# A two-layer hybrid DiT block on one core: the overflow branch, the order of the last two experts, and three adaLN blocks

## The chip, the cores and the metric

The kernel runs on one NeuronCore of a Trainium2 chip. The metric is the device time of one execution in microseconds (us); the time before is the median of three runs.

## What is computed

Two layers (l = 0, 1) run over 256 latent tokens and, in layer 0, 256 context tokens, with D = 1024. Cut to what matters:

```python
for l in range(2):
    mod = silu_c @ w_ada[l] + b_ada[l]                  # adaLN: 6 vectors of 1024, for latent and for context
    u = (x * (1 + sc1) + sh1) @ w_in[l]                 # one projection, 1024 x 4096
    a = hgrn2_mixer(u)                                  # gated linear recurrence, 4 heads, both directions
    b = na_mixer(u)                                     # 2-D neighbourhood attention, 8 heads
    x = layer_norm(ALPHA * x + g1 * (concat(a, b) @ w_out[l]))
    f = grouped_moe(x * (1 + sc2) + sh2)                # 16 experts, 2 per token: silu(t@Wg)*(t@Wu) @ Wd
    x = layer_norm(ALPHA * x + g2 * f)
```

All of it is float32. The adaLN product of a layer is cut into 24 blocks of 256 columns, 1 MB of w_ada each.

## The kernel before

**Layer 0's front** (`front`, L470). The projection is worked off in 16 chunks of 256 columns. The weights of a chunk (1 MB) are loaded by SP into a tile `w8` (`wload`, L194, DMA at L199), and are then split in four pieces into a high and a low float32r half: `wh` by ACT (L421), `wl` by POOL or DVE (L422). TensorE multiplies three products for each piece (L426, L427, L428; the results are named `pscm` where channels lie on the partitions, `pstm` where tokens do). adaLN blocks use the same tiles: a `w8` is loaded from w_ada, and `ada_blocks` (L367) issues 8 matmuls a block into `psada` (L377), an ACT copy (L380), then a transpose pair `ptada` (L384) and two DVE operations (L395). One such group can hold several blocks if they are of the same kind; the kinds change at blocks 8, 12 and 20 of a layer (`fill`, L399). **The ring of `w8` tiles has three buffers (NWP = 3), used in the order of the program**, and SP issues its loads in that order too. How many blocks are worked behind which chunk stands in a table, `FILL0` for layer 0: 18 in all. They go on into the blocks of layer 1 once those of layer 0 are done. After a chunk the attention of finished heads (`ats` L880/L881, `atp` L901, `ato` L912, with `ex` on DVE at L891) and the recurrence (`hgB` L727, `hgX` L744 to L784, `hgt` L661) is worked in between; a scheduler weaves them on TensorE.

**The experts** (`moe`, L1303). Each expert loads gate and up as four tiles of 1 MB (`load(e, "gu")`, half of them for `gu(e, k0)`, half for `gu(e, k1)`) and down as two (`load(e, "d")`), all by SP at L1335. The tiles come from `wslot()`: a ring `we` of seven, later slots of `mw` and others. Tokens are gathered (`xg`, POOL L1345), transposed (`ptx` L1354), multiplied (`pgA` L1369), put through silu and product (L1386 to L1388), transposed (`pth` L1394, `hdT` L1396), multiplied down (`pdA` L1406, `pdB` L1412), copied to `y` (ACT L1419, DVE L1425) and scattered to DRAM as `yD` (POOL L1433). `y` has a single buffer. The loop over the experts works gate and up of expert e + 1 ahead of down of expert e; with `early` set, down of the last but one expert goes between the two halves of the last one's gate and up. `early` holds in layer 1 only.

**Behind the experts.** If an expert got more tokens than it has room for, `overflow(l)` works them off. A flag (DVE maximum L1521, matmul `pfl` L1523, `values_load` L1526) is read by each engine in both layers, and `tc.If(fv)` (L1531) branches at the end of each `moe`. Ahead of this branch, in layer 0, six adaLN blocks of layer 1 are loaded (L1486, NADA = 6): three into `w8` tiles, three into `mw` tiles; `fill(6, True)` works them. Then `combine` (L1535) loads `yD` back (L1555), scales it (ACT L1579, DVE L1580), transposes it (`ptf` L1568) and makes the input of layer 1.

Of the kernel before, what the change touches and what calls it, by code (L numbers as in the profile page):

```python
# [40 lines left out]
NADA = 6  # L41
NFREE = 14, 13
SPL = ({3: "GVGV", 4: "GGVG", 6: "GGVG", 7: "GGVG", 13: "GVGG", 14: "GVGV"}, {1: "VVGV", 2: "VVGV", 3: "VGVG", 4: "GVGG"})
NF, NTOT, NBT = 1, 1, 3
FILL0 = (0, 0, 0, 2, 2, 2, 2, 0, 2, 0, 2, 2, 0, 2, 0, 2)
# [140 lines left out]
class Emit:  # L186
# [55 lines left out]
    def open(self, name, side="left", **k):  # L242
        p = self.tc.tile_pool(name=f"{name}{self.l}", bufs=1, side=side, reuse_waits="tile", **k)
        return p, p.__enter__()
# [17 lines left out]
    def run(self):  # L262
# [48 lines left out]
        self.late = self.open_step = None  # L311
        for l in range(2):
            self.l = l
            self.layer(l)
            if self.stop and self.stop.startswith(f"L{l}"):
                return

# [112 lines left out]
    def layer(self, l):  # L430
        self.t0 = 0 if l == 0 else CTX
        self.T = (NT - self.t0) // P
        psa, self.psA = self.open("psA", space=PSUM)
        psb, self.psB = self.open("psB", space=PSUM)
        if l == 0:
            self.late, self.fp = self.open("late", "left")
            self.xsplit_alloc()
        early, self.tp = self.open("early", "right")
        self.front(l)
        self.close(early)  # L440
        rp, self.rp = self.open("rt", "right")
        we, self.wep = self.open("we", "right")
        self.close(psb)
        self.close(psa)
        psp, self.ps = zip(*(self.open(f"ps{i}", space=PSUM) for i in range(2)))
        self.psA = self.psB = None
        self.rA, self.rB = [0, 1], [3]
        sums = self.w_out(l)
        self.close(self.late)
        moe, self.ep = self.open("moe", "left")  # L450
        self.ln1_end(1, *sums)
        self.moe(l)
        self.close(moe)
        if l == 0:
            self.l = 1
            self.late, self.fp = self.open("late", "left")
            self.xsplit_alloc()
            self.l = 0
            self.combine(l)
        self.close(psp[1])  # L460
        self.close(psp[0])
        self.close(we)
        self.close(rp)
# [6 lines left out]
    def front(self, l):  # L470
# [9 lines left out]
        if l == 0:  # L480
# [6 lines left out]
            def blocks(p):  # L487
                for b in (2 * p, 2 * p + 1):
                    self.todo[b - self.todo[0][1]] = (l, b, self.wload(A["wada"][l, b])[:])
# [34 lines left out]
            def load(p):  # L524
# [6 lines left out]
                if p == 0:  # L531
# [771 lines left out]
    def moe(self, l):  # L1303
# [97 lines left out]
        def down(e):  # L1401
# [12 lines left out]
            y = et([P, D], "y")  # L1414
# [43 lines left out]
        flag = self.rt([P, 1], "flag", 1, I32)  # L1458
        for e in range(NE):
# [3 lines left out]
            early = l == 1 and e == NE - 2  # L1463
# [15 lines left out]
            if e == NE - 1 and l == 0:  # L1479

                for i in range(NADA):
                    if i < NWP:
                        w = self.wp.tile([P, 2048], F32, tag="w8", name="wa")[:]
                    else:
                        w = ep.tile([P, 2, 1024], F32, tag="mw", bufs=NMW, name="wa").rearrange("p a b -> p (a b)")
                    nc.sync.dma_start(w, self.A["wada"][self.todo[i][:2]])  # L1486
                    self.todo[i] = self.todo[i][:2] + (w,)
# [31 lines left out]
            if e == 3:  # L1519
                fl16 = self.rt([P, 1], "fl16", 1, F16)  # L1520
                V.tensor_reduce(fl16[:], R["ov"][:, :T], axis=AX.XY, op=ALU.max)  # L1521
                pfl = self.bank(7, "pfl")
                mm(pfl[:, 0:1], self.one16[:], fl16[:], start=True, stop=True)  # L1523
                V.tensor_copy(flag[:], pfl[:, 0:1])
                fv = nc.values_load(flag[0:1, 0:1], min_val=0, max_val=P)
        if l == 0:  # L1526
            self.rA = self.rB = [4, 5, 6, 7]
            self.fill(NADA, True)
        else:
            self.finish()  # L1530
        with self.tc.If(fv):  # L1531
            self.overflow(l)
# [236 lines left out]
```

## Time and profile before

| | |
|---|---|
| median of three runs | 1316.8 us (1316.08 to 1317.06) |
| profiled execution | 1317.83 us, span 1316.1 us |
| TensorE, VectorE, ScalarE, GpSimd busy | 1199.3, 590.2, 413.8, 334.4 us |
| layer 0: front, w_out and routing, experts | to 367, to 450, to 697 us |
| handover: end of layer 0's experts to layer 1 | 697 to 742 us |
| layer 1: front to routing, experts, end | to 1055, to 1288, to 1316 us |

The stages are read off the timeline of the profiled execution. In the rows below, a row of a timeline gives the start in us, the duration, the engine, the line, the operation with its output and inputs, their shapes and the number of instructions that are taken together; brackets hold the idle time of the engine before it and what ended that. A PE row of float32 counts two passes for each matmul. SPq rows are the DMA issues of SP; several on one line are taken together, from the start of the first to the end of the last.

### The profile page before, as it was taken

The numbers are of one execution on the slowest core, as the hardware profiler recorded it, in microseconds if no ns is written. First come the engines' busy times: TensorE is split into PE (matmuls) and PEld (weight loads), VectorE is DVE, ScalarE is ACT, GpSimd is POOL, SyncE is SP. The second block draws the span as 40 slices with busy tenths as digits, with TensorE's granted clock in tenths as the row PEclk, the third lists the DMA queues.
The fourth block names the chain that finished last, engine by engine and source line by source line (L and its number), as shares of the span: only waits on it lengthen the run. The fifth ranks groups of instructions, "written<-read, shape, count | busy, mean of one in ns | idle before, by whom it ended". The sixth has DMA issues, their size and how long they took to land. (4 is left out here: it accounts for less than half of the span.)

```text
span 1316.1 us, 22763 instructions
## 1 busy us (share of the span) xinstructions
PE 1199.3 (91%) x8919; PEld 747.6 (57%) x8919; DVE 590.2 (45%) x1397; ACT 413.8 (31%) x905; POOL 334.4 (25%) x349
## 2 busy tenths in 40 slices
PE   6989999988999799998997999998889899999984
PEld 4778767667788334333332688876667734333321
DVE  2466554786735414121111756364785524322214
ACT  2233254452544114111112653354345312001011
POOL 2233243323223101111000534353343311111001
PEclk9999999999999799999998999998999889999996
DMA  8794325313385799999998524354335799999993
GB/s 299 250 313 189 122 89 197 116 52 108 124 332 188 266 374 375 386 395 384 412 404 298 227 101 167 115 192 152 131 116 213 314 352 380 389 404 402 421 413 151
DMA packets 67684, 339.32 MB, mean 258 GB/s; under 512 B 10003, under 2 KB 17907, under 8 KB 31856
## 3 DMA queue, kind: packets, MB, share of 16 engines
q1 hardware_dynamic: 54016, 315.74, 62.1%
q0 software_dynamic: 5936, 12.58, 2.9%
q10 hardware_dynamic: 7616, 9.44, 2.2%
q8 instruction: 74, 1.21, 0.4%
q14 instruction: 42, 0.34, 0.1%
HBM read 322.80 MB, written 20.45 MB: 261 GB/s over the span
## 5 line engine op out<-in xcount | busy, mean ns | idle before, releaser
L422 POOL TENSOR_TENSOR wl<-w,wh 128x512 fp32r<-128x512 f32 x121 | 166.4, 1389 | 188.5 <-ACT wh L421 171.7
L1369 PE MATMUL pgA<-we,xgT 128*64 128x512 f32 x688 | 165.2, 613 | 2.7 <-DMA we<-in_wgu_dram 2.7
L426 PE MATMUL pscm<-xh,wh 128*128 128x512 f32 (+1 forms) x320 | 119.1, 376 | 3.3 <-ACT wh L421 2.3
L427 PE MATMUL pscm<-xl,wh 128*128 128x512 f32 (+1 forms) x320 | 120.7, 379 | 0.7 <-POOL xl L1603 0.5
L428 PE MATMUL pscm<-xh,wl 128*128 128x512 f32 (+1 forms) x320 | 118.6, 375 | 2.8 <-POOL wl L422 2.6
L421 ACT ACTIVATE wh<-w 128x512 fp32r<-128x512 f32 x160 | 96.5, 626 | 50.4 <-PE pscm L427 18.7
L1369 PEld LDWEIGHTS pgA<-we,xgT 128*64 128x64 f32 x688 | 48.1, 140 | 95.1 <-issue 84.9
L427 PE MATMUL pstm<-wl,xh 128*128 128x256 f32 x320 | 92.6, 290 | 3.4 <-DVE wl L422 1.8
L428 PE MATMUL pstm<-wh,xl 128*128 128x256 f32 x320 | 91.9, 287 | 0.0
L426 PE MATMUL pstm<-wh,xh 128*128 128x256 f32 x320 | 91.6, 287 | 0.0
L1433 POOL DMA_INDIRECT yD<-y,ss x25 | 23.0, 921 | 244.6 <-DVE y L1421 79.9
L1406 PE MATMUL pdA<-we,hdT 128*64 128x512 f32 x320 | 77.6, 619 | 3.3 <-DMA we<-in_wd_dram 3.2
L1369 PE MATMUL pgA<-mw,xgT 128*64 128x512 f32 x336 | 77.5, 598 | 0.0
L1360 DVE COPY xgT<-ptx 128x256 f32<-128x256 f32 (+1 forms) x32 | 15.4, 482 | 134.2 <-PE ptx L1354 91.1
L426 PEld LDWEIGHTS pscm<-xh,wh 128*128 128x128 f32 x320 | 61.3, 193 | 13.8 <-ACT wh L421 2.4
L428 PEld LDWEIGHTS pscm<-xh,wl 128*128 128x128 f32 x320 | 61.5, 193 | 12.5 <-POOL wl L422 3.4
L427 PEld LDWEIGHTS pscm<-xl,wh 128*128 128x128 f32 x320 | 61.9, 194 | 11.2 <-POOL xl L1603 1.6
L1387 DVE SCALAR_TENSOR_TENSOR hid<-hid,pgA 128x256 f32<-128x256 f32 x32 | 13.5, 421 | 115.2 <-ACT hid L1386 115.1
L427 PEld LDWEIGHTS pstm<-wl,xh 128*128 128x128 f32 x320 | 61.4, 192 | 5.4 <-POOL wl L422 2.2
L1386 ACT ACTIVATE hid<-pgA 128x256 f32<-128x256 f32 x32 | 12.3, 383 | 159.5 <-PE pgA L1369 159.5
L428 PEld LDWEIGHTS pstm<-wh,xl 128*128 128x128 f32 x320 | 61.5, 192 | 1.1 <-issue 0.8
L426 PEld LDWEIGHTS pstm<-wh,xh 128*128 128x128 f32 x320 | 61.4, 192 | 0.5
(394 smaller groups left out, 2358.9 us busy)
## 6 DMA issues: line engine op xcount, KB each, us to landing
we<-in_wgu_dram SPq DMA_DIRECT2D x86, 1024.0 KB
mw<-in_wgu_dram SPq DMA_DIRECT2D x42, 1024.0 KB
w<-in_wada_dram SPq DMA_DIRECT2D x41, 1024.0 KB
we<-in_wd_dram SPq DMA_DIRECT2D x40, 1024.0 KB
w<-in_win_dram SPq DMA_DIRECT2D x29, 1024.0 KB
mw<-in_wd_dram SPq DMA_DIRECT2D x24, 1024.0 KB
w<-in_wout_dram SPq DMA_DIRECT2D x11, 1024.0 KB
wa<-in_wada_dram SPq DMA_DIRECT2D x6, 1024.0 KB
```

What stands on the lines that cost most here:

```text
L421: self.nc.scalar.activation(hi, src, AF.Copy)
L422: leng.tensor_tensor(lo, src, hi.bitcast(F32), op=ALU.subtract)
L426: mm(out, lh, rh, start=first, stop=False, **k)
L427: mm(out, lh, rl, start=False, stop=False, **k)
L428: mm(out, ll, rh, start=False, stop=last, **k)
L1360: V.tensor_copy(t[:, 0:4, :c], src)
L1369: mm(pA[64 * j:64 * j + 64, :], xgT[e][:, k, 0:64], wk[:, 512 * j:512 * j + 512], start=(k == 0), stop=(k == KT - 1), skip_group_check=Tru ...
L1386: S.activation(h, ps[:, :n], AF.Tanh, scale=0.5)
L1387: V.scalar_tensor_tensor(h, h, 1.0, ps[:, :n], op0=ALU.add, op1=ALU.mult)
L1406: mm(dA[64 * j:64 * j + 64, :], hdT[e][:, kb, 0:64], wk[:, 512 * j:512 * j + 512], start=(kb == 0), stop=(kb == 3), skip_group_check=True, ...
L1433: G.indirect_dma_start(out=self.yD[l][:], out_offset=bass.IndirectOffsetOnAxis(ap=idx, axis=0), in_=y[:c], in_offset=None, bounds_check=2 ...
```

## The change

There are four edits.

- The branch at the end of each layer is gone. In layer 0 the DVE maximum of the overflow marks is kept in a tile (`over`); in layer 1 it is joined with that layer's, and one flag is made. Behind both layers one `tc.If` runs the whole pass again, with `slow` set, and only this second pass calls `overflow`.
- `early` holds in both layers: in layer 0, too, down of expert 14 (and the load of its weights) goes ahead of the second half of gate and up of expert 15. The last expert's `y` in layer 0 comes from the ring of two `xg` tiles.
- Behind the experts of layer 0, three adaLN blocks are worked in place of six (NAFTER = 3), and their tiles are `we` tiles.
- The three others are worked in layer 0's front: `FILL0` has 3 in place of 2 behind chunks 8, 11 and 13.

```diff
@@ constants
 NADA = 6
+NAFTER = 3
-FILL0 = (0, 0, 0, 2, 2, 2, 2, 0, 2, 0, 2, 2, 0, 2, 0, 2)
+FILL0 = (0, 0, 0, 2, 2, 2, 2, 0, 3, 0, 2, 3, 0, 3, 0, 2)
@@ run
+        self.over = c([P, 1], "over")
+        self.slow = False
         for l in range(2):
             self.l = l
             self.layer(l)
...
+        with tc.If(self.fv):
+            self.slow = True
+            self.x = [self.xtile(h) for h in range(2)]
+            for l in range(2):
+                self.l = l
+                self.layer(l)
@@ layer
         self.moe(l)
+        if self.slow:
+            self.overflow(l)
@@ moe, down
-            y = et([P, D], "y")
+            y = et([P, D], "xg", NXG) if l == 0 and e == NE - 1 else et([P, D], "y")
@@ moe, loop over the experts
-            early = l == 1 and e == NE - 2
+            early = e == NE - 2
...
-                for i in range(NADA):
-                    if i < NWP:
-                        w = self.wp.tile([P, 2048], F32, tag="w8", name="wa")[:]
-                    else:
-                        w = ep.tile([P, 2, 1024], F32, tag="mw", bufs=NMW, name="wa").rearrange("p a b -> p (a b)")
-                    nc.sync.dma_start(w, self.A["wada"][self.todo[i][:2]])
-                    self.todo[i] = self.todo[i][:2] + (w,)
+                for i in range(NAFTER) if self.todo else ():
+                    t = self.todo[i][:2]
+                    w = self.wep.tile([P, 2, 1024], F32, tag="we", bufs=NWE, name="wa").rearrange("p a b -> p (a b)")
+                    nc.sync.dma_start(w, self.A["wada"][t])
+                    self.todo[i] = t + (w,)
...
-            if e == 3:
+            if e == 3 and l == 0:
+                V.tensor_reduce(self.over[:], R["ov"][:, :T], axis=AX.XY, op=ALU.max)
+            if e == 3 and l == 1 and not self.slow:
                 fl16 = self.rt([P, 1], "fl16", 1, F16)
                 V.tensor_reduce(fl16[:], R["ov"][:, :T], axis=AX.XY, op=ALU.max)
+                V.tensor_tensor(fl16[:], fl16[:], self.over[:], op=ALU.max)
                 pfl = self.bank(7, "pfl")
                 mm(pfl[:, 0:1], self.one16[:], fl16[:], start=True, stop=True)
...
         if l == 0:
             self.rA = self.rB = [4, 5, 6, 7]
-            self.fill(NADA, True)
+            self.fill(NAFTER, True)
         else:
             self.finish()
-        with self.tc.If(fv):
-            self.overflow(l)
```

**SP's loads at chunks 8 to 11 of layer 0.** `in_win` is a chunk, `in_wada` an adaLN block; the number behind `w8_` counts the tiles of the ring, so that tiles whose numbers differ by three share a buffer. Before (chunk 8 is `w8_21`, chunk 9 `w8_24`):

```order
L199 DMA w8_21_1741<-in_win_dram 128x2048
L199 DMA w8_22_1814<-in_wada_dram 128x2048
L199 DMA w8_23_1824<-in_wada_dram 128x2048
L199 DMA w8_24_1841<-in_win_dram 128x2048
L199 DMA w8_25_1947<-in_win_dram 128x2048
L199 DMA w8_26_2021<-in_wada_dram 128x2048
L199 DMA w8_27_2031<-in_wada_dram 128x2048
```

and after (chunk 9 is `w8_25`, and its buffer is that of `w8_22`):

```order
L200 DMA w8_21_1742<-in_win_dram 128x2048
L200 DMA w8_22_1815<-in_wada_dram 128x2048
L200 DMA w8_23_1825<-in_wada_dram 128x2048
L200 DMA w8_24_1835<-in_wada_dram 128x2048
L200 DMA w8_25_1852<-in_win_dram 128x2048
L200 DMA w8_26_1958<-in_win_dram 128x2048
L200 DMA w8_27_2032<-in_wada_dram 128x2048
L200 DMA w8_28_2050<-in_wada_dram 128x2048
```

One block more stands ahead of chunk 9, which moves chunk 9 to the buffer of the group's first block.

**TensorE at chunk 9.** `psada` is the adaLN group behind chunk 8, `ato` attention, `ptada` the transpose pair of the group, and `pscm` chunk 9. Before:

```order
L377 MATMUL psada_1813<-w8_22_1814,scw_89 32x256
L912 MATMUL ato_1592<-pT_1680,bv_0_603 64x256 x7
L377 MATMUL psada_1813<-w8_22_1814,scw_89 32x256 x7
L377 MATMUL psada_1813<-w8_23_1824,scw_89 32x256 x8
L384 MATMUL ptada_1836<-ct_69,adasb_1467 128x4 x2
L426 MATMUL pscm_1859<-xh0_0_118,wh_0_1843 128x512
L427 MATMUL pscm_1859<-xl0_0_126,wh_0_1843 128x512
L428 MATMUL pscm_1859<-xh0_0_118,wl_0_1844 128x512
```

and after:

```order
L387 MATMUL psada_1814<-w8_22_1815,scw_89 32x256
L924 MATMUL ato_1593<-pT_1681,bv_0_604 64x256 x7
L387 MATMUL psada_1814<-w8_22_1815,scw_89 32x256 x7
L387 MATMUL psada_1814<-w8_23_1825,scw_89 32x256 x8
L387 MATMUL psada_1814<-w8_24_1835,scw_89 32x256 x8
L394 MATMUL ptada_1847<-ct_69,adasb_1468 128x4 x2
L436 MATMUL pscm_1870<-xh0_0_119,wh_0_1854 128x512
L437 MATMUL pscm_1870<-xl0_0_127,wh_0_1854 128x512
L438 MATMUL pscm_1870<-xh0_0_119,wl_0_1855 128x512
```

The third block's 8 matmuls are put between the second's and `ptada`; nothing else moves there.

**TensorE at chunk 12.** `psada` is the last block behind chunk 11, `hgB` and `hgX` the recurrence, `ats` attention scores, `pscm` chunk 12. Before:

```order
L377 MATMUL psada_2303<-w8_30_2314,scw_89 32x256 x8
L384 MATMUL ptada_2326<-ct_69,adasb_2041 128x4 x2
L727 MATMUL hgB_2345<-uq_1990,ks_2343 64x64 x8
L744 MATMUL hgX_2358<-Q2_0_2331,KC_2356 64x64 x8
L426 MATMUL pscm_2520<-xh0_0_118,wh_0_2504 128x512
L427 MATMUL pscm_2520<-xl0_0_126,wh_0_2504 128x512
L428 MATMUL pscm_2520<-xh0_0_118,wl_0_2505 128x512
L426 MATMUL pscm_2520<-xh1_0_119,wh_0_2504 128x512
L427 MATMUL pscm_2520<-xl1_0_127,wh_0_2504 128x512
L428 MATMUL pscm_2520<-xh1_0_119,wl_0_2505 128x512
L744 MATMUL hgX_2373<-Q2_0_2331,KC_2371 64x64 x8
```

and after:

```order
L387 MATMUL psada_2322<-w8_32_2343,scw_89 32x256 x8
L394 MATMUL ptada_2355<-ct_69,adasb_2060 128x2 x2
L739 MATMUL hgB_2374<-uq_2001,ks_2372 64x64 x8
L756 MATMUL hgX_2387<-Q2_0_2360,KC_2385 64x64 x8
L892 MATMUL ats_2605<-ks0_0_2300,qs0_0_2259 128x256
L893 MATMUL ats_2605<-kl0_0_2302,qs0_0_2259 128x256
L892 MATMUL ats_2614<-ks1_0_2301,qs1_0_2260 128x256
L893 MATMUL ats_2614<-kl1_0_2303,qs1_0_2260 128x256
L756 MATMUL hgX_2402<-Q2_0_2360,KC_2400 64x64 x8
L436 MATMUL pscm_2549<-xh0_0_119,wh_0_2533 128x512
L437 MATMUL pscm_2549<-xl0_0_127,wh_0_2533 128x512
L436 MATMUL pscm_2576<-xh0_0_119,wh_0_2533 128x512
```

Four attention matmuls now stand where chunk 12 began, and chunk 12 begins behind the second `hgX`. Chunk 14 has moved in the same way behind chunk 13's blocks.

**TensorE at the end of layer 0's experts.** `pgA` with `xgT_0_6335` (before) or `xgT_0_6355` (after) is gate and up of expert 15, `pdA` with two tiles of weights is down of expert 14 and then of 15, `pth` the transposes of expert 15's hidden values, `psada` the adaLN blocks behind them. Before:

```order
L1369 MATMUL pgA_6418<-we_6400,xgT_0_6335 64x512 x4
L1369 MATMUL pgA_6418<-we_6412,xgT_0_6335 64x512 x4
L1369 MATMUL pgA_6418<-mw_6414,xgT_0_6335 64x512 x4
L1369 MATMUL pgA_6418<-mw_6416,xgT_0_6335 64x512 x4
L1406 MATMUL pdA_6449<-mw_6445,hdT_0_6431 64x512 x4
L1394 MATMUL pth_6465<-ct_69,hid_0_6441 128x128 x2
L1406 MATMUL pdA_6449<-mw_6447,hdT_0_6431 64x512 x4
L1406 MATMUL pdA_6486<-mw_6470,hdT_0_6468 64x512 x4
L1406 MATMUL pdA_6486<-mw_6472,hdT_0_6468 64x512 x4
L377 MATMUL psada_6502<-wa_6474,scw_89 32x256 x8
L377 MATMUL psada_6502<-wa_6476,scw_89 32x256 x8
L377 MATMUL psada_6502<-wa_6478,scw_89 32x256 x8
```

and after:

```order
L1381 MATMUL pgA_6442<-we_6420,xgT_0_6355 64x512 x4
L1381 MATMUL pgA_6442<-we_6432,xgT_0_6355 64x512 x4
L1418 MATMUL pdA_6457<-mw_6434,hdT_0_6455 64x512 x4
L1418 MATMUL pdA_6457<-mw_6436,hdT_0_6455 64x512 x4
L1381 MATMUL pgA_6442<-mw_6438,xgT_0_6355 64x512 x4
L1381 MATMUL pgA_6442<-mw_6440,xgT_0_6355 64x512 x4
L1406 MATMUL pth_6485<-ct_69,hid_0_6481 128x128 x2
L1418 MATMUL pdA_6500<-mw_6490,hdT_0_6488 64x512 x4
L1418 MATMUL pdA_6500<-mw_6492,hdT_0_6488 64x512 x4
L387 MATMUL psada_6516<-wa_6494,scw_89 32x256 x8
L387 MATMUL psada_6516<-wa_6496,scw_89 32x256 x8
L387 MATMUL psada_6516<-wa_6498,scw_89 32x256 x8
```

Down of expert 14 has moved ahead of the second half of gate and up of expert 15, and the branch that stood behind the third adaLN block (with three blocks more behind it) is gone. In layer 1, `pfl` has moved behind the first transposes `ptx`.

## Rows read from the trace of the kernel before

**Rows 1.** The page: busy time, share of the span and instructions of each engine.
```profile
PE 1199.3 (91%) x8919; PEld 747.6 (57%) x8919; DVE 590.2 (45%) x1397; ACT 413.8 (31%) x905; POOL 334.4 (25%) x349
```

**Rows 2.** Windows: bounds, length; PE, PEld, DVE, ACT, POOL busy; PEclk; DMA share; GB/s.
```profile
165.00:243.00 78.00, 75.30 (x455) 54.20 (x455) 43.69 (x102) 42.32 (x97) 33.15 (x31) 1.00 0.36 130
243.00:300.00 57.00, 52.39 (x432) 38.66 (x429) 45.21 (x96) 25.46 (x58) 14.10 (x13) 0.97 0.31 105
300.00:367.00 67.00, 60.41 (x538) 51.67 (x537) 44.94 (x103) 31.62 (x77) 22.38 (x33) 0.97 0.31 113
...
697.00:719.00 22.00, 12.76 (x118) 5.21 (x116) 0.92 (x3) 3.65 (x7) 2.40 (x5) 0.82 0.69 245
...
1055.00:1288.00 233.00, 221.97 (x1422) 82.42 (x1422) 60.95 (x137) 27.03 (x70) 27.77 (x33) 0.98 1.00 395
```

**Rows 3.** Timeline of TensorE, 186 to 197: the group behind chunk 8, then chunk 9.
```profile
192.01 1.93 PE L377 MATMUL psada<-w,scw 128*32 128x256 f32 x30
193.87 0.61 PE L384 MATMUL ptada<-ct,adasb 128*128 128x4 f32 x4
194.34 0.48 PE L426 MATMUL pscm<-xh,wh 128*128 128x512 f32 x1
...
194.88 0.40 PE L428 MATMUL pscm<-xh,wl 128*128 128x512 f32 x1
```

**Rows 4.** Timeline of SP's DMA issues, 160 to 260: one chunk's load.
```profile
208.60 0.33 SPq L199 DMA_DIRECT2D w<-in_win_dram  x1
```

**Rows 5.** Timelines of ACT and POOL, 207 to 221: that chunk's split.
```profile
214.36 1.68 ACT L421 ACTIVATE wh<-w 128x512 fp32r<-128x512 f32 x3 [2.19 <-DMA w<-in_win_dram]
...
215.07 5.01 POOL L422 TENSOR_TENSOR wl<-w,wh 128x512 fp32r<-128x512 f32 x4 [5.80 <-PE pscm L428]
```

**Rows 6.** Waits of SP, 60 to 367: us in total, times, longest.
```profile
SPq L199 <- DMA w<-in_win_dram: 41.8, 9, 8.5
```

**Rows 7.** Timeline of TensorE, 240 to 270: recurrence behind chunk 11's blocks.
```profile
244.40 0.84 PE L744 MATMUL hgX<-Q,KC 128*64 128x64 f32 x16
```

**Rows 8.** Timelines of TensorE in the front: the first and last of six idle gaps.
```profile
266.07 0.67 PE L783 MATMUL hgX<-Q,K 128*128 128x256 f32 x2 [1.96 <-DVE K L796]
...
357.25 0.77 PE L661 MATMUL hgt<-ct,ah 128*128 128x128 f32 x4 [1.70 <-DVE ah L658]
```

**Rows 9.** Windows, columns as above: two stretches of the front.
```profile
180.00:196.00 16.00, 14.21 (x97) 9.29 (x97) 11.65 (x20) 8.46 (x17) 8.27 (x8) 1.00 0.21 66
...
262.00:278.50 16.50, 13.52 (x74) 11.05 (x72) 12.97 (x26) 7.50 (x19) 4.41 (x3) 0.90 0.19 65
```

**Rows 10.** Timeline of all engines, 684 to 720: the end of layer 0's experts.
```profile
693.39 0.38 ACT L1386 ACTIVATE hid<-pgA 128x256 f32<-128x256 f32 x1 [6.50 <-PE pgA L1369]
...
695.47 0.38 ACT L1396 ACTIVATE hdT<-pth 128x256 f32<-128x256 f32 x1 [1.69 <-PE pth L1394]
...
698.64 3.65 PE L1406 MATMUL pdA<-mw,hdT 128*64 128x512 f32 x16 [1.34 <-ACT y L1419]
698.87 0.90 POOL L1433 DMA_INDIRECT yD<-y,ss  x1 [9.07 <-ACT y L1419]
...
704.01 1.19 ACT L1419 ACTIVATE y<-pdA 64x512 f32<-64x512 f32 x2 [5.42 <-DMA yD<-y,ss]
705.48 0.90 POOL L1433 DMA_INDIRECT yD<-y,ss  x1 [5.72 <-ACTq L1531]
...
712.60 5.16 SPq L1555 DMA_DIRECT2D y<-yD  x8
...
717.57 0.72 ACT L1579 ACTIVATE y<-y,gt 128x512 f32<-128x512 f32 x1 [2.36 <-DMA y<-yD]
```

**Rows 11.** The same timeline: TensorE behind the branch.
```profile
709.26 5.49 PE L377 MATMUL psada<-wa,scw 128*32 128x256 f32 x48 [4.24 <-PEq L1531]
```

**Rows 12.** Windows, columns as above: behind the last scatter's issue.
```profile
705.00:710.00 5.00, 0.76 (x12) 0.45 (x12) 0.00 (x0) 0.21 (x1) 0.90 (x1) 0.77 0.92 343
```

**Rows 13.** Timeline of all engines, 1046 to 1058: the flag of layer 1.
```profile
1056.13 0.19 PE L1523 MATMUL pfl<-fl,one 128*128 128x1 f16 x1 [2.75 <-DVE fl L1521]
```

More of the change, by code (lines that the diff above doesn't have):

```diff
@@ L242, in open @@
     def open(self, name, side="left", **k):
-        p = self.tc.tile_pool(name=f"{name}{self.l}", bufs=1, side=side, reuse_waits="tile", **k)
+        p = self.tc.tile_pool(name=f"{name}{self.l}{'s' * self.slow}", bufs=1, side=side, reuse_waits="tile", **k)
         return p, p.__enter__()
@@ L487, in blocks @@
             def blocks(p):
-                for b in (2 * p, 2 * p + 1):
+                for b in (2 * p, 2 * p + 1) if self.todo else ():
                     self.todo[b - self.todo[0][1]] = (l, b, self.wload(A["wada"][l, b])[:])
@@ L530, in load @@
                     nc.sync.dma_start(sub(raw[c], 2 * p), A["win"][l, c][:, 2 * p:2 * p + 2])
-                if p == 0:
+                if p == 0 and self.todo:
                     self.todo[1] = (l, 1, self.wload(A["wada"][l, 1])[:])
@@ L1457, in moe @@
         gu(0, k1)
-        flag = self.rt([P, 1], "flag", 1, I32)
         for e in range(NE):
@@ L1518, in moe @@
                     nc.sync.dma_start(self.ln2[:, i], self.A["ln2"][i:i + 1, :].partition_broadcast(P))
-            if e == 3:
+            if e == 3 and l == 0:
+                V.tensor_reduce(self.over[:], R["ov"][:, :T], axis=AX.XY, op=ALU.max)
+            if e == 3 and l == 1 and not self.slow:
                 fl16 = self.rt([P, 1], "fl16", 1, F16)
                 V.tensor_reduce(fl16[:], R["ov"][:, :T], axis=AX.XY, op=ALU.max)
+                V.tensor_tensor(fl16[:], fl16[:], self.over[:], op=ALU.max)
                 pfl = self.bank(7, "pfl")
                 mm(pfl[:, 0:1], self.one16[:], fl16[:], start=True, stop=True)
+                flag = self.cp.tile([P, 1], I32, name="flag")
                 V.tensor_copy(flag[:], pfl[:, 0:1])
-                fv = nc.values_load(flag[0:1, 0:1], min_val=0, max_val=P)
+                self.fv = nc.values_load(flag[0:1, 0:1], min_val=0, max_val=P)
         if l == 0:
             self.rA = self.rB = [4, 5, 6, 7]
-            self.fill(NADA, True)
+            self.fill(NAFTER, True)
         else:
             self.finish()
-        with self.tc.If(fv):
-            self.overflow(l)
     def combine(self, l):
```

## The prediction

> **What bounds the kernel now.** I read the page first: TensorE is busy 91% of the span [rows 1]. So I cut the span into stages and read each one's busy times, granted clock and DMA share [rows 2]. In layer 0's front, 165 to 367, TensorE is busy 75.30 of 78, 52.39 of 57 and 60.41 of 67 us with the DMA engines at about a third: work put on TensorE here lengthens the stage, and a load is late only where its buffer came free late. At the handover between the layers, 697 to 719, TensorE is busy 12.76 of 22 us: a chain of scatter, landing and load sets the pace. The experts of layer 1 run with the DMA engines full (1.00). Then I read, on the timelines, the three places where the change works: the front of layer 0 (three adaLN blocks come in), the handover (three go out, the branch goes, the last experts are turned round) and the start of layer 1's experts (the flag).
>
> The sum is made against the profiled execution, 1317.8 us; the median is 1316.8, so 1.0 is taken off at the end. About 0.2%, or 2.6 us, is what a measurement of this kernel can tell from no change: "same" is 1314.2 to 1319.4.
>
> **Part 1: three blocks more in layer 0's front.** 30 passes of psada take 1.93 us [rows 3], 0.064 each; a block is 8 matmuls in two passes each, 1.03. Three blocks: **+3.1**, on the bound engine. At chunk 10 two blocks now fall into different kinds, so one more transpose pair stands on TensorE, by the row of ptada 0.61: **+0.6**. The small ACT and DVE operations of that group lie beside TensorE's work.
>
> The larger cost is a wait that before does not have. Projection chunks and adaLN blocks share one ring of three buffers (w8). Before, a chunk behind a group of two blocks takes the buffer of the chunk ahead of them, and its load waits for that chunk's split alone; chunk 9's first matmul stands at 194.34 with no idle time ahead of it [rows 3]. After, the third block takes that buffer, and chunk 9 the first block's: its load waits until that block's matmuls are done. The order of the change shows only the two other blocks and a transpose pair between. Block one is done at about 193.0 (192.01 and half of the 30 passes). What a load takes from issue to use shows where one runs alone: issued 208.60 [rows 4], first split 214.36 [rows 5], 5.76, and this split is three for 1.68, so about 0.6 each; the first matmul needs one. 193.0 + 5.76 + 0.6 = 199.4, while TensorE is ready at 194.34 + 1.03 = 195.4: 4.0. The lower half is four for 5.01 on POOL [rows 5], 1.25, and the third matmul asks for it 0.54 behind the first (194.88 against 194.34): 0.7 more. **+4.7**. Bounds: the loads that SP itself waited for took 41.8/9 = 4.6 on the mean and 8.5 at most [rows 6], so 4.6 + 0.6 - 2.4 = 2.8 and 8.5 + 0.6 - 2.4 + 0.7 = 7.4 (2.4 is 195.4 - 193.0). I take the lone load, since the queues are as empty here.
>
> Chunk 12 stands so behind chunk 11's blocks, chunk 14 behind chunk 13's; there the new order has recurrence between: two blocks 2.06, ptada 0.5, three groups hgB and hgX at about 0.7 (0.84 with the tail [rows 7]), four attention matmuls of 256 columns like psada's 0.13, 0.5. That covers 5.2 of 6.4, so 1.2 or 1.3 each: **+2.6**. Bounds 0 (these loads go a little sooner than the others) and 6 (that work slides behind the wait).
>
> What is given back: later in the front TensorE stands idle for DVE or POOL, six times, 1.96 in the first and 1.70 in the last, together 7.7 [rows 8]. Work that is late anyway shortens a gap only where what it waits for was not held up by TensorE too; most of these are DVE results of a projection chunk, which come later as well. I take a third, **-2.7**; bounds 0 and -7.7.
>
> [...]
> [...]
>
> Front: 3.1 + 0.6 + 4.7 + 2.6 - 2.7 + 1.7 = **+10.0**.
>
> **Part 2: the handover.** TensorE does 24 block matmuls here in place of 48, and meets no branch, but neither is on the path: what it must do next are transposes of y, which wait for DVE. The branch held TensorE 4.24 us [rows 11], while the path went through DMA. On the path is the last expert's output. Its ACT copy waits 5.42 us for the scatter of the expert before, because both use one buffer; its scatter is issued at 705.48; SP's first load of y goes at 712.60, when that has landed [rows 10]. After, the last expert has another buffer and the expert before it is finished first. So the last gate/up half ends later by one down projection: 693.39 + 3.65 = 697.0. The chain from there to the transposed hidden values, 693.39 to 695.47 + 0.38, 2.46, was beside a down projection and now lies open: 699.5. Down 3.65: 703.15. The ACT copy starts at 703.2 in place of 704.01: -0.8. The last scatter landed 6.2 us after the end of its issue (706.38 to 712.60), the one before it 4.2 (699.77 to 704.01): beside the last ran two adaLN loads of 1 MB that SP issued behind the branch, with the DMA share at 0.92 [rows 12]. After, no such load is left for then: -2.0. Together **-2.8**. Bounds: -0.8 (landing unchanged) and -5.2 (and the whole of the 2.36 that ACT waits for the load of y [rows 10]). I take the middle one, since it has a measured pair of landings.
>
> **Part 3: the flags.** pfl leaves its place ahead of layer 1's first ptx, where TensorE waited 2.75 us for it [rows 13]; ptx could go up to 1.8 sooner. But the stage behind is DMA-bound [rows 2] and its loads are released elsewhere: **-0.3**, bounds 0 and -1.8. Layer 0's flag matmul, the DVE maximum added and the single branch at the end cost nothing: other work of the experts hides the first two, and the branch stands at the end either way.
>
> **Sum.** 10.0 - 2.8 - 0.3 = +6.9; 1317.8 + 6.9 - 1.0 = **1323.7**.
>
> **The rivals.**
> *Same (about 1316).* The front's waits only move idle time: all 7.7 us [rows 8] come back and no clock falls. 3.1 + 0.6 + 4.7 + 2.6 - 7.7 - 2.8 - 0.3 = +0.2, 1317.0; with chunks 12 and 14 covered, 1314.4. For it: the new order puts attention matmuls into the recurrence. Against it: five of the six gaps wait for DVE chains that begin with TensorE results.
> *Faster (1313).* One mechanism, the empty queue at the handover: scatter and load of y both land without the adaLN loads beside them, -5.2. It decides from the point where the front's net cost is under 2.9; at 2.0 it gives 2.0 - 5.2 - 0.3 = -3.5. For it: the chain at 697 to 719 is all DMA latency, at a DMA share of 0.92. Against it: the front must lose less than the 3.7 of its bare matmuls.
> [...]
> *The flag is set.* Then the whole pass runs again, over 2600. TensorE goes from the branch to psada [rows 11] with nothing of the overflow between, so layer 0's flag is clear.
>
> **How the numbers follow.** Forecast, 1319.5 to 1326: 0.44. Clock, above that: 0.15. Same: 0.20. Faster: 0.20. Rerun: 0.01. Slower is 0.44 + 0.15 + 0.01 = 0.60. The range takes in the forecast, the same, most of the clock's case and the near half of the faster: 1312.5 to 1329.
>
> **What would show it.** A stop of about 4 us on TensorE behind three psada blocks at about 195, ended by chunk 9's split or its load; SP waiting for psada there; two stops under 2 us near the recurrence of chunks 12 and 14; a clock below 1.00 behind the first. At the handover, the first load of y about 2.8 us sooner, reckoned from the last expert's first gate/up matmuls, and no branch before the end. It is wrong if the front from 165 to 367 grows by less than 4 us, or if the handover shrinks by more than 5.

## The result: 19 us slower, beyond the range

| | before | changed |
|---|---|---|
| median | 1316.9 us (4 runs, 1316.08 to 1319.82) | 1335.9 us (4 runs, 1330.42 to 1339.20) |
| the same pair again, in another session | 1315.2 us (13 runs) | 1335.3 us (4 runs) |
| profiled execution, first and second trace: span | 1316.1, 1315.2 us | 1328.5, 1333.0 us |

The ratio is 1.0136 (95% interval 1.0099 to 1.0173), in the second session 1.0146 (1.0090 to 1.0202). The forecast was 1323.7 with a range up to 1329. The sign was right; the size was not.

The views that answer to [rows 2] are windows of the changed kernel's trace. The columns are bounds, length, busy time and count of PE, PEld, DVE, ACT and POOL, granted clock, DMA share and GB/s. The stretches are cut at the same events in every kernel: the second group of recurrence matmuls in layer 0, the third, the first matmul of w_out, the first expert, and then the handover from the last expert's first gate and up matmul to the first transposes of y, layer 1's front, and TensorE's last matmul to the end.

```profile
122.80:249.10 126.30, 119.40 (x847) 88.08 (x847) 65.28 (x155) 52.44 (x118) 35.84 (x36) 0.96 0.39 140
249.10:372.10 123.00, 104.83 (x910) 83.76 (x909) 80.50 (x177) 52.38 (x121) 36.54 (x38) 0.96 0.34 118
...
704.70:735.80 31.10, 19.59 (x123) 7.03 (x120) 3.51 (x9) 4.58 (x9) 3.32 (x6) 0.85 0.50 180
813.70:1017.50 203.80, 187.26 (x1493) 150.13 (x1489) 131.00 (x294) 87.01 (x193) 84.56 (x80) 0.99 0.41 148
1312.30:1328.50 16.20, 0.00 (x0) 0.00 (x0) 6.53 (x14) 2.48 (x4) 2.10 (x2) 0.50 0.19 71
```

The same stretches of the kernel before, cut anew:

```profile
125.00:243.90 118.90, 113.78 (x811) 84.84 (x810) 68.34 (x153) 53.61 (x119) 41.85 (x40) 0.99 0.39 144
243.90:358.00 114.10, 103.52 (x894) 82.29 (x893) 83.12 (x177) 51.15 (x119) 31.63 (x35) 0.97 0.27 92
...
686.30:719.20 32.90, 23.48 (x171) 8.69 (x167) 3.52 (x9) 5.21 (x10) 3.32 (x6) 0.88 0.79 298
795.80:1005.40 209.60, 191.89 (x1493) 152.74 (x1489) 131.83 (x294) 87.14 (x193) 84.65 (x80) 0.97 0.40 144
1303.70:1316.10 12.40, 0.04 (x1) 0.00 (x0) 6.23 (x11) 2.18 (x4) 2.10 (x2) 0.50 0.24 88
```

Layer 0's front takes 249.3 us instead of 233.0: **+16.3**. Length less TensorE's busy time is its idle time: 5.1 + 10.6 = 15.7 before, 6.9 + 18.2 = 25.1 after, so +9.4 of it is idle and +6.9 busy. Of the busy part 3.7 is the work that was moved in, by the forecast's count; the other 3.2 goes with the lower granted clock (0.96 in both halves, against 0.99 and 0.97). The handover is 1.8 shorter (31.1 against 32.9), and the end, from TensorE's last matmul, is **3.8 longer** (16.2 against 12.4). Layer 1's front is shorter by 5.8, with the same code; the experiments below show that as chance.

On TensorE's timeline the stop that was forecast stands behind chunk 8's three blocks. The columns are start, duration, engine, line, operation, count, and in brackets the idle time before it with what ended it:

```profile
187.58 2.79 PE L387 MATMUL psada<-w,scw 128*32 128x256 f32 x46
...
194.15 0.80 PE L436 MATMUL pscm<-xh,wh 128*128 128x512 f32 x1 [3.24 <-ACT wh L431]
194.75 0.63 PE L437 MATMUL pscm<-xl,wh 128*128 128x512 f32 x1
```

The stop is 3.24 us, and the matmuls behind it take 0.63 us instead of 0.39; the granted clock of 194.1 to 200.3 is 0.50, where that of 187.5 to 190.4, over the three blocks ahead of the stop, is 1.00. SP's row shows why: chunk 9's load goes at 188.70, when the first of the three blocks (16 of the 48 passes that end at 190.30) is done.

```profile
188.70 1.19 SPq L200 DMA_DIRECT2D w<-in_win_dram  x2
```

Further on, TensorE stops where before had none, at the attention matmuls ahead of chunks 12 and 14, and the last gap of [rows 8] has doubled:

```profile
253.31 0.36 PE L892 MATMUL ats<-ks,qs 128*128 128x256 f32 x1 [2.47 <-ACT wh L431]
```

```profile
310.50 0.55 PE L892 MATMUL ats<-ks,qs 128*128 128x256 f32 x1 [2.96 <-DMA ks<-ks]
```

```profile
371.31 1.09 PE L673 MATMUL hgt<-ct,ah 128*128 128x128 f32 x4 [3.40 <-DVE ah L670]
```

### The profile page after: what moved, and what is told of

It reads as the page before. It is cut to its first block, busy times and chain, and to the rows that moved or that the text cites. A ratio compares the mean times of both kernels' runs of the same rounds, so it can differ in the third digit from the quotient of the medians.

```text
span 1328.5 us, 22740 instructions
## 1 busy us (share of the span) xinstructions
PE 1197.8 (90%) x8922; PEld 749.4 (56%) x8922; DVE 584.3 (44%) x1399; ACT 414.0 (31%) x906; POOL 332.1 (25%) x349
## 5 line engine op out<-in xcount | busy, mean ns | idle before, releaser
L437 PEld LDWEIGHTS pscm<-xl,wh 128*128 128x128 f32 x320 | 61.9, 194 | 11.4 <-POOL xl L1614 1.6
L1399 DVE SCALAR_TENSOR_TENSOR hid<-hid,pgA 128x256 f32<-128x256 f32 x32 | 13.5, 421 | 120.5 <-ACT hid L1398 120.4
```

What stands on the lines that cost most here:

```text
L437: mm(out, lh, rl, start=False, stop=False, **k)
L1399: V.scalar_tensor_tensor(h, h, 1.0, ps[:, :n], op0=ALU.add, op1=ALU.mult)
```

## The experiments

Theory A: the third block of a group takes the buffer that the next chunk's load needs, so chunks 9, 12 and 14 come late, and the stops and the clock behind them make the loss. Rivals: the second pass in the program or the new order costs it (B), or any three blocks more cost it (C).

**All three blocks back.**

```diff
-FILL0 = (0, 0, 0, 2, 2, 2, 2, 0, 3, 0, 2, 3, 0, 3, 0, 2)
+FILL0 = (0, 0, 0, 2, 2, 2, 2, 0, 2, 0, 2, 2, 0, 2, 0, 2)
-NAFTER = 3
+NAFTER = 6
```

> The changed kernel with the three adaLN blocks moved back: FILL0 as before, six blocks behind layer 0's experts, all in we tiles. Nothing else is undone (no branch between the layers, the new order of the last experts stay). Theory A (the three blocks in the front make chunks 9, 12 and 14 wait for their own group's first block): the whole loss goes, 1313 to 1318 us, and TensorE from 165 to the end of the front takes about the 202 us of before instead of 219. Rival B (the second pass in the program, the new order or the missing branch costs it): it stays above 1326.

Measured: 1316.5 us (10 runs) where before had 1315.8 (21 runs); ratio 1.0011 (0.9985 to 1.0038). The front is 230.8 us. So the loss hangs on the blocks. But nothing is gained either, though the handover is shorter (30.3 us); the end is 15.9 us in place of 12.4, and the run without the second pass (below) shows why.

**The blocks alone, in the kernel before.** There `FILL0` is that of the change, and three blocks are loaded and worked behind the experts, in the w8 tiles as before.

> The kernel before with the table FILL0 of the change and three blocks behind the experts, their tiles as before; branch, flag and order of the experts are those of before. Theory A: 1330 to 1340 us, with stops of 2.5 to 3.3 us on TensorE at chunk 9 and at the recurrence of chunks 12 and 14, and a spread between its runs of several us, since the clock falls behind the stops. Rival B: 1316 to 1320, within 0.2% of before plus the 3.1 us of the blocks' own matmuls.

Measured: 1327.5 us (6 runs), ratio 1.0093 (1.0061 to 1.0124), which is below the range of A and far above that of B. Windows of its front, handover and end:

```profile
122.40:371.60 249.20, 224.91 (x1753) 172.25 (x1753) 146.39 (x332) 105.10 (x238) 72.40 (x74) 0.95 0.36 129
703.90:731.90 28.00, 18.37 (x122) 6.87 (x118) 3.51 (x9) 4.88 (x10) 3.33 (x6) 0.88 0.66 237
1311.30:1323.50 12.20, 0.00 (x0) 0.00 (x0) 6.22 (x11) 1.85 (x4) 2.10 (x2) 0.50 0.24 89
```

The front costs the full 249.2 us without any other part of the change. What keeps the total lower is that its handover is 28.0 and its end 12.2: with three adaLN blocks behind the experts, the old order and the branch between the layers, the handover is shorter than the changed kernel's 31.1. That pointed to a new wait in the changed kernel.

**The same 21 blocks, spread.**

```diff
-FILL0 = (0, 0, 0, 2, 2, 2, 2, 0, 3, 0, 2, 3, 0, 3, 0, 2)
+FILL0 = (0, 0, 0, 2, 2, 2, 2, 1, 2, 1, 2, 2, 1, 2, 0, 2)
```

> The changed kernel with the three moved blocks put singly behind chunks 7, 9 and 12, which had none, instead of as third blocks behind chunks 8, 11 and 13: the same 21 blocks in the front, but no chunk's load takes the buffer of a block of the group right ahead of it. Theory A (the ring): only the bare work is left, 3.1 us of matmuls and some transpose pairs at 0.6, so 1317 to 1324, and no stop of over 2 us at chunks 9, 12 and 14. Rival C (three more blocks cost this wherever they stand in the front): 1330 to 1340.

Measured: 1323.9 us (10 runs), ratio 1.0059 (1.0034 to 1.0084). The front is 236.7 us, 3.6 above the 233.1 of before's second trace: the bare work. (Against the 230.8 of the kernel with all blocks back it is 5.9; fronts with the old table lie at 230.8 to 233.1.) Behind chunk 8's blocks TensorE goes on without a stop, at 0.39 us a matmul where the changed kernel has 0.63:

```profile
197.03 0.48 PE L436 MATMUL pscm<-xh,wh 128*128 128x512 f32 x1
197.34 0.39 PE L437 MATMUL pscm<-xl,wh 128*128 128x512 f32 x1
```

So C falls: the same blocks cost 3.6 us here, and 16.3 where they stand as third blocks. Their place makes 12 to 13 of the 16; how much of that is the ring itself, the runs below divide only in part.

**A buffer of its own for expert 14's output.** In the changed kernel's handover, ACT's copy of expert 14's `y` waits for the scatter of expert 13, since these two still share the single `y`, and the silu of expert 15 is queued behind it on ACT. The timeline of all engines there:

```profile
711.60 3.60 PE L1381 MATMUL pgA<-mw,xgT 128*64 128x512 f32 x16
716.07 1.20 ACT L1431 ACTIVATE y<-pdA 64x512 f32<-64x512 f32 x2 [11.03 <-DMA yD<-y,ss]
717.29 0.38 ACT L1398 ACTIVATE hid<-pgA 128x256 f32<-128x256 f32 x1
...
718.73 0.41 PE L1406 MATMUL pth<-ct,hid 128*128 128x128 f32 x2 [3.52 <-DVE hid L1400]
...
719.61 5.29 PE L1418 MATMUL pdA<-mw,hdT 128*64 128x512 f32 x16 [0.47 <-ACT hdT L1408]
...
726.47 0.90 POOL L1445 DMA_INDIRECT yD<-xg,ss  x1 [8.03 <-ACT xg L1431]
...
729.65 4.95 SPq L1566 DMA_DIRECT2D y<-yD  x8
```

Gate and up end at 715.2, and the silu starts at 717.29. TensorE's stop of 3.52 us is followed by a down projection at 5.29 us where 3.65 is usual [rows 10].

```diff
-y = et([P, D], "xg", NXG) if l == 0 and e == NE - 1 else et([P, D], "y")
+y = et([P, D], "xg", NXG) if l == 0 and e >= NE - 2 else et([P, D], "y")
```

> The changed kernel with the output y of expert 14 in layer 0, too, in the ring of the xg tiles, so that its copy does not wait for the scatter of expert 13 on the single y tile (ACT waited 11.03 us for it, and expert 15's silu is queued behind that copy on ACT). Theory D (this wait ate the gain of the handover): TensorE's 3.5 us of idle ahead of expert 15's transposes falls to about 2, the first load of y goes 3 to 5 us sooner after the experts, and the time falls by as much against the changed kernel: about 1331 to 1333 where that has 1336. Rival E (the handover is set by the transfers anyway): no change, within 1 us.

Measured: 1331.6 us (4 runs), ratio to before 1.0111 (1.0075 to 1.0148), in the range of theory D; beside the changed kernel's 1335.3 and 1335.9 that is about 4 less, though the intervals overlap. The trace decides: ACT's wait is gone, TensorE stops for 1.49 us, the down projection is back at 3.65, and the handover is 27.5 us.

```profile
716.85 0.38 ACT L1398 ACTIVATE hid<-pgA 128x256 f32<-128x256 f32 x1 [1.90 <-PE pgA L1381]
...
718.29 0.41 PE L1406 MATMUL pth<-ct,hid 128*128 128x128 f32 x2 [1.49 <-DVE hid L1400]
...
719.17 3.65 PE L1418 MATMUL pdA<-mw,hdT 128*64 128x512 f32 x16 [0.47 <-ACT hdT L1408]
```

**One block only.**

```diff
-FILL0 = (0, 0, 0, 2, 2, 2, 2, 0, 3, 0, 2, 3, 0, 3, 0, 2)
+FILL0 = (0, 0, 0, 2, 2, 2, 2, 0, 3, 0, 2, 2, 0, 2, 0, 2)
-NAFTER = 3
+NAFTER = 5
```

> The changed kernel with only one of the three blocks moved (the third block behind chunk 8; the other two are worked behind layer 0's experts again, five there). Theory A: one stop of about 3.2 us at chunk 9 and the matmuls behind it at half clock, no stops at chunks 12 and 14; the front to the start of w_out is longer than that of the kernel with all blocks moved back by 1.0 + 3.2 + about 3.4 for the clock = 6 to 8 us of the 16 to 18, so 1321 to 1325 in all. If the rest (9 us) still stands, the cause lies elsewhere in the front.

Measured: 1324.2 us (6 runs), ratio 1.0055 (1.0024 to 1.0085). The front's two halves:

```profile
125.20:250.20 125.00, 118.11 (x830) 87.56 (x829) 65.48 (x155) 54.13 (x121) 40.98 (x40) 0.96 0.39 145
250.20:362.90 112.70, 101.27 (x898) 80.44 (x897) 82.87 (x180) 50.95 (x119) 32.73 (x34) 0.99 0.31 107
```

Against the kernel with all blocks back (118.2 and 112.6) the first half is 6.8 longer, as expected, and the second is not longer at all. The 6.8 is about what its parts give: 1.0 for the block's matmuls, 3.24 for the stop (the same in this trace) and the 2.5 that the next run finds for the clock. First halves with two blocks there lie between 118.2 and 120.5, so the sum is good to 2 us. The other two blocks then make 123.0 - 112.7 = 10.3 us there, of which 6.8 is idle (18.2 against 11.4).

**Covering the stop.** Behind the group of chunk 8, 24 idle matmuls into an unused half of the bank fill the time in which TensorE waits for chunk 9.

```diff
             self.flush()
+            if m == 3 and self.l == 0 and self.cnk == 8:
+                ps, w = self.last
+                for r in range(24):
+                    g = 32 * (r % 4)
+                    self.nc.tensor.matmul(ps[g:g + 32, 256:512], self.scw[:, r % KT, 0:32], w[:, r % KT, :], ...)
             self.open_step = new
```

> The changed kernel with 24 idle matmuls (48 passes, 3.1 us, into an unused half of psada's bank) put on TensorE right behind the group of chunk 8, where it stops for chunk 9's load. The load comes no sooner, so the first matmul of chunk 9 starts within 0.5 us of where it did against psada's start (6.6 us behind it). Theory F (the clock's fall behind the stop costs as much as the stop): chunk 9's first sixteen matmuls then run at 0.39 us instead of 0.63, the stretch to chunk 10's first matmul is 2.5 to 3.5 us shorter, and the total 2 to 4 us below the changed kernel. Rival G (the 0.63 comes from late operands or from the split beside it, not from the stop): no change there.

Measured: 1335.2 us (4 runs, 1326.09 to 1338.31), ratio 1.0130 (1.0086 to 1.0174): in the total no difference can be told, so the 2 to 4 us expected there did not show. The stretch shows it:

```profile
190.30 2.79 PE L388 MATMUL psada<-w,scw 128*32 128x256 f32 x46
...
197.01 0.50 PE L443 MATMUL pscm<-xh,wh 128*128 128x512 f32 x1 [0.63 <-ACT wh L438]
197.35 0.39 PE L444 MATMUL pscm<-xl,wh 128*128 128x512 f32 x1
```

Chunk 9 starts 6.71 us behind the psada group (6.57 in the changed kernel), so no sooner, but at 0.39 us a matmul. The half from the second to the third recurrence is 123.8 us at a clock of 0.99, against 126.3 at 0.96 (126.4 in the changed kernel's second trace). So 2.5 us of chunk 9's price was the clock, as theory F has it, at the low end of its range; rival G falls. In the traced execution (1336.85 us) layer 1's front hides it: 212.1 us, 8.3 more than the changed kernel's with the same code. The other three executions have no trace.

**The versions without the new waits.** First all blocks back and own tiles for both last outputs; then all blocks back and the old order of the last two experts.

> The three blocks moved back behind layer 0's experts, as in the first run of this study, and the outputs of experts 14 and 15 of layer 0 both in the ring of the xg tiles. If the stop of the copy for the scatter was what ate the handover's gain, the stretch from expert 15's first gate and up matmul to the first transposes of y is 27 to 28.5 us instead of 30.3 (32.9 before), and the time is 1311 to 1314 us where before has 1315.8: faster than both kernels. If the handover is worth nothing whatever is done there, 1315 to 1317.

> The three blocks moved back and the order of the last two experts as before (down of 14 behind gate and up of 15); the last expert's output stays in the xg ring, the branch stays gone, six blocks in we tiles. It has no stop of ACT for expert 13's scatter and none of TensorE for expert 15's silu. If the new order is what costs, the stretch from expert 15's first gate and up matmul to the first transposes of y is 27.5 to 29 us and the time 1312 to 1315; if the new order helps by the 0.8 us that was forecast, the stretch is 30.5 to 32 us and the time 1316 to 1318.

Measured: 1315.6 us (12 runs), ratio 1.0007 (0.9988 to 1.0027), and 1316.7 us (10 runs), ratio 1.0014 (0.9988 to 1.0040). The windows of the handover are 29.0 and 29.3 us, shorter than before's, though each lies just above its expected range. With the extra wait gone the two orders of the experts differ by 0.3 us, less than the handover of one program differs between two traces (32.9 and 34.7), so no worth of the new order is shown. Both totals missed their ranges of 1311 to 1314 and 1312 to 1315. In both the end is 16 us, and the 3 us or so by which it is longer there eat most of the handover's gain.

**Both kernels again**, for a second trace of each.

> The kernel before once more, for a second trace of the same program. Layer 1's front (from its first recurrence to its projection w_out) took 209.6 us in the first trace and 203.8 to 212.1 in the traces of the others, where that code is the same. Theory H (chance: whether the clock falls behind its stops of about 2 us differs from run to run): 203 to 212, not the same value again, and the stretch from w_out to the first expert of layer 0, 88.7 in the first trace and 89.9 to 92.4 in the others, may change too. Rival I (the kernel's layout sets it): both within 0.5 us of the first trace.

> The changed kernel once more, beside the kernel before, for more runs and a second trace. Theory A and H: the front of layer 0 between its second recurrence and w_out is 249 us again within 1 (233.0 before), the handover 31 within 1, while layer 1's front may lie anywhere from 203 to 212; the median 1331 to 1337.

Windows of before's second trace (front, handover, end), then of the changed kernel's (front, handover, end):

```profile
125.40:358.50 233.10, 217.11 (x1701) 166.84 (x1700) 151.68 (x330) 104.75 (x238) 73.10 (x75) 0.98 0.33 118
690.20:724.90 34.70, 24.27 (x170) 8.79 (x166) 3.52 (x9) 4.88 (x10) 3.31 (x6) 0.81 0.74 277
...
1302.00:1315.20 13.20, 0.01 (x1) 0.00 (x0) 7.36 (x16) 2.48 (x4) 2.10 (x2) 0.63 0.23 84
```

```profile
127.80:377.50 249.70, 225.16 (x1754) 172.30 (x1753) 146.16 (x332) 104.95 (x238) 72.52 (x74) 0.95 0.36 129
709.30:740.60 31.30, 19.64 (x123) 7.04 (x120) 3.51 (x9) 4.68 (x10) 3.32 (x6) 0.85 0.50 183
1316.50:1333.00 16.50, 0.00 (x0) 0.00 (x0) 6.67 (x14) 2.48 (x4) 2.10 (x2) 0.50 0.19 70
```

Fronts repeat within 0.4 us, handovers within 2, ends within 0.8. Layer 1's front in the same program is 209.6 at a clock of 0.97 once and 205.3 at 0.99 the other time, so theory H holds there. The stretch from w_out to the first expert differs as well: before it is 88.6 us in the first trace and 92.2 in the second, and 92.2 in both of the changed kernel.

**The change without its new waits, blocks spread.**

> The three blocks singly behind chunks 7, 9 and 12, and the outputs of experts 14 and 15 both in the xg ring: what is left of the change without its two new waits. Front 236 to 238 us (233.0 before), handover 27 to 29 (32.9 before). By the sum of both, 1315 to 1319; if the front's bare work shows in full as in the first run with the spread blocks, 1319 to 1323. It does not beat the kernel before by more than 0.2% in either case.

Measured: 1318.1 us (10 runs), ratio 1.0032 (1.0005 to 1.0058): front 236.4, handover 27.5, as expected, and still not faster than before.

**Without the second pass.** The `tc.If` behind both layers and its body are left out; the flag is still made and read.

> The changed kernel without its second pass: the flag is still made and read by every engine, but the branch and the rerun behind it are left out (so overflowing tokens would be lost; the flag is clear for these inputs). In the traces so far the time from TensorE's last matmul to the end of the span is 12.2 to 13.2 us in the three traces with the branch of before (before twice, blocks alone) and 15.9 to 16.7 in all those with the single branch at the end. Theory J (passing over the second pass holds POOL, whose drain then ends last, by about 3.5 us): 11 to 13.5 us here, and the total 3 to 4 us below the changed kernel, 1331 to 1333; the front keeps its 249 us. Rival K (something else of the change lengthens the end): 16 again.

Measured: 1329.1 us (4 runs), ratio 1.0108 (1.0074 to 1.0141), about 6 below the changed kernel's medians of other sessions, and 2 below the expected range. The front is 249.5 us, as expected. The end is 12.0 us:

```profile
1316.30:1328.30 12.00, 0.04 (x1) 0.00 (x0) 6.23 (x11) 1.89 (x4) 2.10 (x2) 0.50 0.24 88
```

So theory J holds for the end, and rival K falls; the rest of the six lies within the intervals. What POOL's sequencer does at the end, in the changed kernel (line L321 is the branch, L1776 the program's end; the columns are operation, count, duration in ns as least, median and most, and first and last start):

```profile
L321 POOLq EVENT_SEMAPHORE  x5: 17/42/43, 1320.3 to 1320.6; - x5
...
L321 POOLq COMPARE_BRANCH  x1: 58/58/58, 1317.7 to 1317.7; - x1
...
L321 POOLq INC_SWDGE_SEM  x1: 1444/1444/1444, 1320.7 to 1320.7; - x1
```

```profile
L1776 POOLq DRAIN  x3: 46/107/5219, 1322.2 to 1328.3; - x3
```

and in the kernel before:

```profile
L1531 POOLq COMPARE_BRANCH  x2: 54/54/54, 705.8 to 1308.7; - x2
...
L1531 POOLq EVENT_SEMAPHORE  x1: 17/17/17, 1309.6 to 1309.6; - x1
```

```profile
L1765 POOLq DRAIN  x3: 46/107/5219, 1309.7 to 1315.8; - x3
```

The drain of 5.22 us is the same. Before, it starts at 1309.7, 1.0 us behind the branch; POOL's last operation ends at 1309.58, so the branch lay beside it and cost nothing. After, the drain starts at 1322.2, 4.5 us behind the branch and 3.8 behind POOL's last operation, which ends at 1318.40: 2.6 until the first instruction behind the branch, and 1.9 for more semaphores and an operation of 1.44 us that before does not have. Without the second pass the drain starts at 1320.6, beside POOL's last operation (1320.65 to 1322.17), and takes 6.80 us. In all three traces the program ends about 1 us after this drain. The first instruction comes 2.6 us behind the branch over the whole second pass and 0.9 behind that over one overflow routine; that the length of the jump makes the difference, no run shows.

**Before, with the loads early.**

```diff
-                    if i < NWP:
-                        w = self.wp.tile([P, 2048], F32, tag="w8", name="wa")[:]
-                    else:
-                        w = ep.tile([P, 2, 1024], F32, tag="mw", ...)
+                    w = self.wep.tile([P, 2, 1024], F32, tag="we", bufs=NWE, name="wa").rearrange("p a b -> p (a b)")
...
-            y = et([P, D], "y")
+            y = et([P, D], "xg", NXG) if l == 0 and e == NE - 1 else et([P, D], "y")
```

> The kernel before, with two things of the change that its runs speak for: the six adaLN blocks behind layer 0's experts have we tiles (so that all six loads go ahead of SP's branch), and the last expert's output of layer 0 has an xg tile. Order of the experts, branches, flag and front are those of before. Front 233, end 12 to 13, handover 27.5 to 30 us in place of 32.9 and 34.7: 1309 to 1313 where before has 1315 to 1316, so faster than both by 0.2 to 0.4%. If the branch itself sets the handover, 32 to 34 us and no change.

Measured: **1313.0 us** (12 runs) where before had 1316.6 (17 runs); ratio 0.9981 (0.9965 to 0.9998). The handover:

```profile
688.20:717.80 29.60, 22.44 (x171) 8.91 (x168) 3.52 (x9) 4.87 (x10) 3.33 (x6) 0.94 0.78 297
```

```profile
708.07 0.90 POOL L1433 DMA_INDIRECT yD<-xg,ss  x1 [6.36 <-issue]
...
711.28 5.98 SPq L1552 DMA_DIRECT2D y<-yD  x8
```

29.6 us with the branch in place, where all blocks back in the old order, without it, had 29.3: the missing branch was not what shortens the handover. Of the two things that were changed, the rows speak for the early loads. The last scatter goes 19.9 us behind the window's start (19.2 and 20.1 in before's traces), so the own tile gained nothing; from the end of its issue to the first load of y pass 2.3 us, in place of 6.2 and 7.4. What holds that scatter back once its tile is free, the trace does not name. This version is the fastest of all, by a margin that its interval just clears.

## Why the prediction was right and wrong

**Right.** The bare work of the three blocks, 3.7: 3.6 measured by spreading them. The wait on the ring at chunk 9: 4.0 forecast for the stop, 3.24 measured, released by that chunk's split. The place and the sign of the main loss, and that the branch is off the handover's path (29.6 us with it). The flag: in layer 1 the first gate and up matmul starts 4.90 us behind the last group of `ptb` (the matmuls ahead of `ptx`) in place of 5.26, so 0.4 sooner where 0.3 was forecast; whether that reaches the end no run shows.

**Wrong, step "chunk 12 and 14" and step "what is given back".** Together they were put at 2.6 - 2.7, about nothing. In the second half of the front TensorE's idle time grew by 6.8 us for these two blocks. The estimate counted only the load against the work between, and took four attention matmuls as part of that work. Two of them stood still for 2.47 and 2.96 us, because their keys were still on the way: the copy `ks<-ks` is issued on ACT's queue at 303.72 and used at 310.50.

```profile
303.72 0.47 ACTq L876 DMA_DIRECT2D ks<-ks  x1
```

At 253.31 the releaser is named as ACT's `wh`, but these matmuls do not read it, and the same copy was issued at 247.04, 6.3 us earlier. In the changed kernel's second trace the same stop names the copy, issued there at 252.20:

```profile
258.64 0.35 PE L892 MATMUL ats<-ks,qs 128*128 128x256 f32 x1 [2.65 <-DMA ks<-ks]
```

Before, chunk 12's matmuls stood in that place, and the next attention matmul stood at 263.02, almost 20 us behind that copy's issue (243.45). So work moved into a gap brought its own wait along. The ring's wait was there as well: the splits of chunks 12 and 14 start at 252.65 and 309.91, so that their first pieces, at 0.6 us each, are ready just as the keys land. Had the keys been there, two attention matmuls and a group `hgX` (1.06 us, from 253.31 to 254.37) could have stood ahead of the stops, which leaves 1.4 and 1.9 us for the ring, where 1.2 and 1.3 were forecast. This is an estimate; no run has the one wait without the other. Behind the first stop the recurrence then waits for DVE, 1.23 us at 256.56 and 1.69 at 260.52, where before its groups did not wait.

Nothing was given back: the gaps of [rows 8] make 7.7 us again. The first shrank from 1.96 to 1.00 and two short ones closed, but the last grew from 1.70 to 3.40.

**Wrong, the 1.7 for the clock.** This term of the front's sum was the author's estimate, and no run shows it. What the runs show: the busy time of the front grew by 3.2 us beyond the work moved, at a granted clock of 0.96 in both halves against 0.99 and 0.97; behind chunk 9 alone the covered stop shows 2.5. Not every stop paid: in the first trace the granted clock is 1.00 behind the stop of 2.47 us (253.3 to 257.0) and 0.50 behind that of 2.96 (310.5 to 316.0); in the second it is 0.60 and 0.63 behind the same two.

**Right in size by luck: the handover.** -2.8 was forecast and -1.8 and -3.4 measured (31.1 and 31.3 against 32.9 and 34.7). Two terms were off, one each way. The landing of the last scatter gained more than the 2.0: 727.37 to 729.65 is 2.3 us, against 6.2. But the last scatter goes 21.8 us behind the window's start instead of 19.2, 2.6 later where 0.8 sooner was forecast. The step "the last gate/up half ends later by one down projection" left out what is queued ahead of the silu on ACT: expert 14's copy. Freeing it gave 3.6 us.

**Wrong, step "the single branch at the end cost nothing".** It costs 3.5 us (16.2 and 16.5 against 12.4 and 13.2; 12.0 without it). The sentence compared one branch with one branch. It did not look at what each engine has to do behind it, nor whether the engine is still busy when it branches.

**The sum from what was measured**: front +16.4, handover -2.6, end +3.5, by the means of two traces each: +17.3, against 18.9 and 20.1 between the medians. The missing 2 to 3 us are not located: the two traced executions of the changed kernel lie below the medians (1330.42 and 1334.76), and the slower ones have no trace. Their mean granted clock is lower, 0.947 to 0.952 against 0.954 and 0.955, so lost clock is the likely place. Of the 10.4 us by which these measured terms exceed the forecast's +6.9, the front has 6.4 and the end 3.5.

## What to carry to other kernels

In a ring that is shared by two kinds of loads, count the buffers between one use and the next before adding a member: with three buffers, chunk 9 came without a stop behind two blocks and with one of 3.24 us behind three, and three third blocks cost 16 us of front for 3.7 us of work. When a stop is to be filled with other work, check that this work's own inputs have landed, and check what is queued behind a delayed wait on the same engine, as expert 15's silu was behind the 11.03 us that ACT's copy waited. A branch at the very end cost nothing here while its engine was still at work (the end is 12.4 and 13.2 us with it, 12.0 without any), and about 3.5 us where POOL's drain of 5.22 us came behind it.

## What the runs showed of the hardware

**Identical code differs by almost 9 us.** Layer 1's front took 203.2 to 212.1 us in these traces. TensorE's granted clock was 0.96 in the longest (the covered stop's trace, 808.30 to 1020.40) and 0.99 in the changed kernel's 203.8. The kernel before spreads from 1307.3 to 1322.8 over 21 runs, far wider than its first three, and its mean granted clock goes from 0.970 in the shortest of them to 0.956 in the longest; a stage's length tells more than one total.

**The same DVE operations differ by 1.07 us beside POOL.** The same two DVE operations take 3.43 us in the first trace of before and 4.50 in the kernel with all blocks back, where POOL's split starts 1.53 us behind their start instead of 1.77, and so ahead of the second of them instead of behind its start:

```profile
399.09 3.43 DVE L1227 TENSOR_TENSOR t<-iota,q 128x1536 f16<-128x1536 f16 x2
```

```profile
400.86 4.01 POOL L422 TENSOR_TENSOR wl<-w,wh 128x512 fp32r<-128x512 f32 x2 [7.74 <-ACT wh L421]
```

```profile
397.71 4.50 DVE L1239 TENSOR_TENSOR t<-iota,q 128x1536 f16<-128x1536 f16 x2
```

```profile
399.24 4.10 POOL L432 TENSOR_TENSOR wl<-w,wh 128x512 fp32r<-128x512 f32 x2 [7.50 <-ACT wh L431]
```

On POOL the pair of splits takes 4.0 to 4.1 us in both, where four take 5.01 elsewhere [rows 5]. What sets these times the traces do not name.
